# Inverting softmax sums once per query: a row through DRAM in place of four reciprocals on 64 partitions

## The chip, the cores and the metric

The kernel runs on one core of a Trainium2 chip. Its engines are named as in the profile: PE does the matrix products (PEld is its weight load), DVE, ACT and POOL work on tiles in on-chip memory, and each of SP, ACT and POOL can issue DMA transfers. Every engine takes its instructions in the order in which they stand in its own queue. An instruction that waits holds all those behind it on that engine. The metric is device time in microseconds (us) for one execution of the whole layer.

## The reference

One encoder layer runs over 2048 prompt tokens and over 256 sample tokens (18 token tiles of 128). What matters here is the attention half of its mixer. Eight heads of 64 dimensions share two key/value heads, and every query attends to all keys of its own request:

```python
def block(qi):
    s = jnp.einsum('bqhgd,bkhd->bhgqk', qi, k).astype(jnp.float32) * scale
    p = jax.nn.softmax(s, axis=-1)
    return jnp.einsum('bhgqk,bkhd->bqhgd', p.astype(v.dtype), v)
```

Beside it, eight other heads run the mLSTM, a recurrence over chunks of 64 tokens in both directions. The two results go together through `w_out` into the residual, and a gated feed-forward layer with a depthwise convolution follows.

## The kernel before

**Attention in blocks.** `attention` goes over 36 blocks (`hbs`) of 512 queries. A block is named by its first head and first query tile: `1_0` is head 1 from query tile 0. Blocks `0_16`, `2_16`, `4_16` and `6_16` are small ones, for the 256 sample tokens (two heads at once, one pair of key tiles). The other 32 cover the prompt, with eight pairs of key tiles each. The first half of the list (`0_16` to `3_12`) uses key/value head 0, the second half (`4_0` to `6_14`) head 1.

**A pair of key tiles.** `scores` makes the product of keys and queries in a PSUM bank (`ps`, lines 616 and 617). ACT takes the exponential twice, once rounded (`ph`, line 620) and once in full (line 621), and DVE subtracts them into the remainder `pl` (line 622). `values` (line 634) multiplies `ph` and `pl` with the values and adds up over the pairs in one PSUM bank `pv`. The value tiles carry 64 columns of ones, so partitions 64 to 127 of `pv` hold the same softmax sum, 64 times over. `values` lags `scores` by two pairs (`PLAG`). The next block's row maxima are found meanwhile: `maxstep` makes scores (`px`, line 590) that DVE reduces (`mx`, line 591). The banks of `ps`, `px` and two smaller users are shared, four in all (tag `sc`), and `pv` has one buffer.

**The end of a block.** After a block's last pair, `fin1` copies the output (`o1`, line 642) and the 64 copies of the sums (`rs`, line 643) out of `pv` on ACT. `fin2`, four times, inverts 128 columns of `rs` on all 64 partitions (line 651, DVE). `fin3` multiplies the two on POOL (line 655) and stores the result to DRAM (`mix_d`, line 658). `rs` has one buffer, so the next block's `fin1` waits for this block's `fin3`. The six steps stand in the list `fins`; one is taken out after each pair of the next block, two after its last pair, and what is left is flushed ahead of the next `fin1`.

**The mLSTM beside it.** `mlstm` works through four pairs of heads. Its projections are line 780, 790 and (last pair) 808 on PE, from tiles `mn`, `mjn` or `mvn` that SP loads from DRAM (lines 777 and 805) into a ring of eight buffers: a load waits until PE has read the tile that lay there before. Its output steps, one for each of 18 token tiles and each pair of heads, go back and forth between engines: `mS` (PE, line 911), `dm` (DVE, 914), `mI` and `mN` (PE, 917 and 929), `s`, `dn` and `hh` (DVE, 920 to 949, with a square sum on ACT, line 941, and a power on POOL, 104 and 105), `mT` (PE, 954) and `mmx` (957 to 960), which is stored to `mix_d`.

**What sets the order.** `run_both` draws from the two generators by a table of costs. The framework then reorders each engine's queue: it simulates the program with its own idea of durations, and takes the earlier written instruction where several are ready. So a step that it believes shorter can move instructions everywhere in this stretch. Once the mLSTM's generator is exhausted, which falls into block `4_8`, PE's order is taken as written instead: attention and the output projection `phase_c` (`po`, line 1069, from tiles `cmx`) alternate by a fixed pace. After attention follow the feed-forward stages.

Of the kernel before, what the change touches and what calls it, by code (L numbers as in the profile page):

```python
# [9 lines left out]
F32 = mybir.dt.float32  # L10
F32R = mybir.dt.float32r
AF = mybir.ActivationFunctionType
# [5 lines left out]
P = 128  # L18
# [6 lines left out]
HD = 64  # L25
# [468 lines left out]
def attention(g, tc, s1, s2, pp):  # L494


    nc = g.nc
    sp = s1
# [43 lines left out]
    def part(s):  # L542

        t, r = 0, []
        for q in s.qs:
            r.append((t, q))
            t += q[2] - q[1]
        return r
# [77 lines left out]
    def values(s, kp, parts):  # L626

        N = s.N
        if kp == 0:
            s.pv = pp.tile([P, 512], F32, tag="pv", name="pv" + s.nm, bufs=1)  # L630
        vs = [[v[:, (2 * kp + z) % 4, :] for v in s.kv[kp // 2][2]] for z in range(2)]
        todo = [(vs[z][k], parts[z][0]) for z in range(2) for k in range(2)] + [(vs[z][0], parts[z][1]) for z in range(2)]
        for k, (v, p) in enumerate(todo):
            nc.tensor.matmul(s.pv[0:HD if k in (1, 3) else P, 0:N], v, p, start=(kp == 0 and k == 0),  # L634
                             stop=(2 * kp + 2 == s.nk and k == 5))

    def fin1(s):

        N = s.N
        s.o1 = sp.tile([HD, 512], F32, tag="o1", name="o1" + s.nm, bufs=2)  # L640
        s.rs = sp.tile([HD, 512], F32, tag="rs", name="rs" + s.nm, bufs=1)
        nc.scalar.activation(s.o1[:, 0:N], s.pv[0:HD, 0:N], AF.Copy)
        nc.scalar.activation(s.rs[:, 0:N], s.pv[HD:P, 0:N], AF.Copy)
        s.left = list(range(0, N, P))

    def fin2(s):

        if s.left:
            r = s.rs[:, s.left[0]:s.left[0] + P]
            s.left.pop(0)  # L650
            nc.vector.reciprocal(r, r)

    def fin3(s):
        N = s.N
        nc.gpsimd.tensor_tensor(s.o1[:, 0:N], s.o1[:, 0:N], s.rs[:, 0:N], ALU.mult)
        for t0, (h, q0, q1) in part(s):
            r0 = HD * (h % 2)
            nc.gpsimd.dma_start(g.mix_d[q0 // 2:q1 // 2, r0:r0 + HD, 4 + h // 2].rearrange("n p t -> p n t"),
                                s.o1[:, t0 * P:(t0 + q1 - q0) * P].rearrange("p (n t) -> p n t", t=BT))

    def fin4(s):

        for h, q0, q1 in s.qs:
            if h == 7:
                g.mixed.update(range(q0, q1))
# [12 lines left out]
    todo, fins = [], []  # L678

    def value():  # L680

        s, kp, parts = todo.pop(0)
        values(s, kp, parts)
        if kp == s.nk // 2 - 1:
            while fins:
                fins.pop(0)()
            fin1(s)
            fins.extend([lambda: fin2(s)] * 4 + [lambda: fin3(s), lambda: fin4(s)])

    for n in range(len(hbs)):  # L690
        nxt = prep(n + 1) if n + 1 < len(hbs) else None
# [3 lines left out]
        for kp in range(nkp):  # L695
            todo.append((cur, kp, scores(cur, kp)))
            yield 0.4 * A_PAIR
            if ready:
                prep2b(ready)
                ready = None  # L700
            if nxt is not None and nxt.todo:
                if n == len(hbs) // 2 - 1:

                    k = 2 * (kp - 2) - (nxt.nq * nxt.nsp - len(nxt.todo))
                else:
                    k = -(-len(nxt.todo) // max(nkp - kp - (MXZ if g.alone else MXE), 1))
                for i in range(k):
                    maxstep(nxt)
                    if i % 2:
                        yield 2 * A_MAX  # L710
                if not nxt.todo:
                    prep2a(nxt)
                    ready = nxt
            if len(todo) > PLAG:
                value()
                yield 0.6 * A_PAIR
            for _ in range(1 if kp < nkp - 1 else 2):
                if fins:
                    fins.pop(0)()
# [9 lines left out]
    while todo:  # L729
        yield A_PAIR  # L730
        value()
# [866 lines left out]
def body(tc, aps, phases="abcd"):  # L1598
    nc = tc.nc
    g = Ctx()  # L1600
# [3 lines left out]
    with ExitStack() as st:  # L1604
        dp = st.enter_context(tc.tile_pool(name="dram", bufs=1, space=DRAM))
# [5 lines left out]
        def dram(name, shape):  # L1611
            setattr(g, name, dp.tile(shape, F32, name=name))
# [7 lines left out]
        dram("q_d", [NT, P, 8, P])  # L1620
        dram("k_d", [2, P, T])
        dram("v_d", [2, 2, P, NT, HD])
        dram("nm_d", [NT, 17, P])
        dram("og_d", [4, NB, P, 2, P])
        g.ident = kp.tile([P, P], F32, name="ident")
# [177 lines left out]
```

## Time and profile before

| | |
|---|---|
| median of 3 runs | 3366.88 us (3366.43 to 3368.13) |
| profiled execution | 3374.1 us, its span 3372.4 us |
| granted PE clock, mean over the span | 0.986 of full |
| busy share of PE, DVE, ACT, POOL | 97%, 71%, 53%, 39% |
| first and last `rs` copy of attention (line 643) | 252.25 and 1773.25 us |
| copies of `rs` of blocks `1_0`, `6_6`, `4_16`, `6_16`, `4_8` | 377.70, 1368.14, 1374.44, 1421.09, 1465.53 us |

The spans of instructions are the hardware profiler's. PE's instructions overlap one another, so PE can be shown busy while it could take more. "Idle before" is the time that an engine stood still ahead of an instruction, with the instruction that ended it. Times in this document are microseconds unless marked ns.

### The profile page before, as it was taken

The numbers are of one execution on the slowest core, as the hardware profiler recorded it, in microseconds if no ns is written. First come the engines' busy times: TensorE is split into PE (matmuls) and PEld (weight loads), VectorE is DVE, ScalarE is ACT, GpSimd is POOL, SyncE is SP. The second block draws the span as 40 slices with busy tenths as digits, with TensorE's granted clock in tenths as the row PEclk, the third lists the DMA queues.
The fourth block names the chain that finished last, engine by engine and source line by source line (L and its number), as shares of the span: only waits on it lengthen the run. The fifth ranks groups of instructions, "written<-read, shape, count | busy, mean of one in ns | idle before, by whom it ended". The sixth has DMA issues, their size and how long they took to land. (4 is left out here: it accounts for less than half of the span.)

```text
span 3372.4 us, 57131 instructions
## 1 busy us (share of the span) xinstructions
PE 3271.5 (97%) x21366; PEld 3047.6 (90%) x21366; DVE 2403.1 (71%) x3727; ACT 1802.4 (53%) x3781; POOL 1327.6 (39%) x1686
## 2 busy tenths in 40 slices
PE   8899999999999999899999999999999999999998
PEld 6788888888888888788889999999999998999998
DVE  7875687777768788876766778877877776544573
ACT  5545666667666777665552544445555555323331
POOL 8652133213333323211246457645554442851112
PEclk9999999999999999999999999999999999999999
DMA  8765343343336444433347334424322223885563
GB/s 273 229 201 150 94 126 97 105 125 98 113 108 188 130 135 128 123 99 96 103 133 263 129 102 148 127 96 176 107 93 97 100 93 102 302 274 172 164 223 107
DMA packets 300636, 483.03 MB, mean 143 GB/s; under 512 B 36597, under 2 KB 186279, under 8 KB 300359
## 3 DMA queue, kind: packets, MB, share of 16 engines
q1 hardware_dynamic: 247543, 348.34, 32.8%
q0 software_dynamic: 36256, 121.60, 10.8%
q10 hardware_dynamic: 16560, 9.44, 0.9%
q8 instruction: 168, 2.75, 0.3%
q14 instruction: 109, 0.89, 0.1%
HBM read 337.37 MB, written 141.91 MB: 142 GB/s over the span
## 5 line engine op out<-in xcount | busy, mean ns | idle before, releaser
L622 DVE TENSOR_TENSOR pl<-ps,ph 128x512 fp32r<-128x512 f32 x520 | 354.0, 685 | 202.1 <-ACT ps L621 190.3
L1226 PE MATMUL pa<-nt,wut 128*128 128x290 f32 (+1 forms) x3168 | 449.2, 298 | 8.7 <-ACT u L1244 8.6
L620 ACT ACTIVATE ph<-ps 128x512 fp32r<-128x512 f32 x520 | 310.0, 596 | 265.7 <-PE ps L617 253.1
L1226 PEld LDWEIGHTS pa<-nt,wut 128*128 128x128 f32 x3168 | 433.1, 190 | 10.9 <-ACT u L1244 10.6
L591 DVE TENSOR_REDUCE mx<-px 128x1 f32<-128x512 f32 (+1 forms) x528 | 346.5, 674 | 100.0 <-PE px L590 98.0
L1336 DVE SCALAR_TENSOR_TENSOR y<-u,cw,y 128x1152 f32<-128x1152 f32 (+1 forms) x176 | 325.3, 1848 | 39.2 <-ACT yc L1334 17.5
L634 PE MATMUL pv<-ph,v 128*128 128x512 f32 (+1 forms) x1040 | 319.4, 402 | 0.8 <-ACT ph L620 0.3
L621 ACT ACTIVATE ps<-ps 128x512 f32<-128x512 f32 x520 | 310.3, 597 | 0.0
L1555 PE MATMUL et<-tet,wet 128*128 128x384 f32 x1584 | 279.0, 336 | 0.0
L1555 PEld LDWEIGHTS et<-tet,wet 128*128 128x128 f32 x1584 | 277.1, 188 | 0.0
L1069 PEld LDWEIGHTS po<-cmx,wo 128*128 128x128 f32 x1728 | 221.6, 191 | 9.6 <-DVE cmx L1057 1.5
L1069 PE MATMUL po<-cmx,wo 128*128 128x256 f32 x1728 | 225.8, 284 | 1.5 <-DVE cmx L1057 1.3
L1555 PE MATMUL e<-te,we 128*128 128x384 f32 x1188 | 213.9, 341 | 11.0 <-ACT te L1397 7.1
L1555 PEld LDWEIGHTS e<-te,we 128*128 128x128 f32 x1188 | 211.5, 191 | 12.0 <-ACT te L1397 7.3
L616 PE MATMUL ps<-qq,kk 128*128 128x512 f32 x520 | 215.9, 417 | 6.0 <-DVE mx L591 3.8
L780 PE MATMUL mj<-mn,wm 128*128 128x256 f32 x1296 | 200.8, 289 | 9.7 <-DMA mn<-n_d 3.9
L780 PEld LDWEIGHTS mj<-mn,wm 128*128 128x128 f32 x1296 | 185.5, 194 | 26.6 <-issue 6.8
L617 PE MATMUL ps<-qm,kl 65*128 65x512 f32 x520 | 207.6, 401 | 0.0
L590 PE MATMUL px<-kk,qq 128*128 128x512 f32 (+1 forms) x528 | 203.2, 415 | 3.9 <-DVE mx L591 2.6
L790 PEld LDWEIGHTS mv<-wm,mn 128*128 128x128 f32 x1296 | 181.9, 190 | 17.8 <-ACT qb L786 2.3
L790 PE MATMUL mv<-wm,mn 128*128 128x256 f32 x1296 | 194.8, 285 | 0.9 <-ACT qb L786 0.8
L634 PE MATMUL pv<-pl,v 128*128 128x512 f32 x520 | 192.2, 401 | 0.0
(307 smaller groups left out, 7216.9 us busy)
## 6 DMA issues: line engine op xcount, KB each, us to landing
mn<-n_d SPq DMA_DIRECT2D x216, 256.0 KB, 3.4
ru<-w_up SPq DMA_DIRECT2D x88, 512.0 KB, 3.6
a_d<-y POOLq DMA_DIRECT2D x88, 288.0 KB, 2.6
a_d<-tc POOLq DMA_DIRECT2D x66, 288.0 KB, 2.8
n_d<-n1T SPq DMA_DIRECT2D x18, 1024.0 KB, 5.7
dm<-nm_d POOLq DMA_DIRECT2D x72, 256.0 KB, 4.0
mjn<-n_d SPq DMA_DIRECT2D x72, 256.0 KB, 3.5
mvn<-n_d SPq DMA_DIRECT2D x72, 256.0 KB, 3.1
```

Source lines behind the costliest of these rows:

```text
L591: nc.vector.tensor_reduce(s.mx[:, t, z0:z0 + 1], ps[:, 0:w], AX.X, ALU.max)
L616: nc.tensor.matmul(ps, kk[:, kc:kc + P], s.qq[:, 0:N], start=True, stop=False)
L620: nc.scalar.activation(ph, ps, AF.Exp)
L621: nc.scalar.activation(ps, ps, AF.Exp)
L622: nc.vector.tensor_tensor(pl, ps, f32(ph), ALU.subtract)
L634: nc.tensor.matmul(s.pv[0:HD if k in (1, 3) else P, 0:N], v, p, start=(kp == 0 and k == 0), stop=(2 * kp + 2 == s.nk and k == 5))
L780: nc.tensor.matmul(pj[:, o], s.w[c][:, a, o * P:(o + 1) * P], nT[c][:, :, h, :], start=(c + o + k == 0), stop=(c == NCC - 1 and k == 2 and ...
L790: nc.tensor.matmul(pv[:, o], nT[c][:, o, a, :], s.w[c][:, h, 256:512], start=(c + o + k == 0), stop=(c == NCC - 1 and k == 2 and o == 1))
L1069: nc.tensor.matmul(po[:, o], wo[z // 2][c][:, a, n], mx[c][:, h, :], start=(c == 0 and k == 0), stop=(c == NCC - 1 and k == 2))
L1226: nc.tensor.matmul(p[:, z], w[:, aa, c, :], ops[k][:, c, bb, z * m:z * m + m], start=c == 0 and i == 0 and not add, stop=c == NCC // 2 - 1 ...
L1336: nc.vector.scalar_tensor_tensor(y[:, s:e], u[:, s + k:e + k], cw[:, k, jj:jj + 1], y[:, s:e], ALU.mult, ALU.add)
L1555: nc.tensor.matmul(ps[m // 2][:, m % 2], w[:, aa, m * P:(m + 1) * P], t[:, bb], start=p == 0 and n == 0, stop=p == NP - 1 and n == 2)
```

## The change

`fin1` now copies one partition of the sums instead of 64. The four `fin2` steps are replaced by four others. `fin2a` writes the row of 512 sums to DRAM; `fin2b` reads it back as 64 partitions by 8; `fin2c` inverts that tile with one DVE instruction and writes it to a second row in DRAM; `fin2d` reads that row to all 64 partitions of `rs`. The four transfers stand on SP's queue, and each waits for the one before. `fin3` and `fin4` are as they were, and there are again six steps in `fins`. Every block has a DRAM tile of its own (`g.rs_d`, 36 of them).

```diff
         nc.scalar.activation(s.o1[:, 0:N], s.pv[0:HD, 0:N], AF.Copy)
-        nc.scalar.activation(s.rs[:, 0:N], s.pv[HD:P, 0:N], AF.Copy)
-        s.left = list(range(0, N, P))
-
-    def fin2(s):
-
-        if s.left:
-            r = s.rs[:, s.left[0]:s.left[0] + P]
-            s.left.pop(0)
-            nc.vector.reciprocal(r, r)
+        nc.scalar.activation(s.rs[0:1, 0:N], s.pv[HD:HD + 1, 0:N], AF.Copy)
+        s.row = g.rs_d.pop(0)
+
+    def fin2a(s):
+
+        nc.sync.dma_start(s.row[0].unsqueeze(0), s.rs[0:1, :])
+
+    def fin2b(s):
+
+        s.rr = sp.tile([HD, 8], F32, tag="rr", name="rr" + s.nm, bufs=2)
+        nc.sync.dma_start(s.rr, s.row[0].rearrange("(p f) -> p f", f=8))
+
+    def fin2c(s):
+
+        nc.vector.reciprocal(s.rr, s.rr)
+        nc.sync.dma_start(s.row[1].rearrange("(p f) -> p f", f=8), s.rr)
+
+    def fin2d(s):
+
+        nc.sync.dma_start(s.rs, s.row[1].unsqueeze(0).to_broadcast([HD, 512]))
...
-            fins.extend([lambda: fin2(s)] * 4 + [lambda: fin3(s), lambda: fin4(s)])
+            fins.extend([lambda f=f: f(s) for f in (fin2a, fin2b, fin2c, fin2d, fin3, fin4)])
...
+        g.rs_d = [dp.tile([2, 512], F32, name=f"rs_d{k}") for k in range(36)]
```

The change also moves what it does not name, since the framework plans anew. Line numbers behind line 643 are larger by 11 or 12 in the changed kernel (line 808 is its line 819, line 777 its line 788).

On DVE, at the end of block `1_0` (with the first pairs of block `2_0`, and the maxima of block `3_0`), there stood before:

```order
L622 TENSOR_TENSOR pl2_0_0_1_3983<-ps2_0_0_1_3979,ph2_0_0_1_3982 128x512
L877 SCALAR_TENSOR_TENSOR C0_14_2475<-C0_13_2474,dec_137,C0_14_2475 128x65
L591 TENSOR_REDUCE mx3_0_3970<-px3_0_0_0_3987 128x1
L591 TENSOR_REDUCE mx3_0_3970<-px3_0_1_0_3990 128x1
L651 RECIPROCAL rs1_0_4180<-rs1_0_4180 64x128 x4
L591 TENSOR_REDUCE mx3_0_3970<-px3_0_2_0_3993 128x1
L591 TENSOR_REDUCE mx3_0_3970<-px3_0_3_0_3996 128x1
L622 TENSOR_TENSOR pl2_0_1_0_4149<-ps2_0_1_0_4145,ph2_0_1_0_4148 128x512
```

and now:

```order
L591 TENSOR_REDUCE mx3_0_4012<-px3_0_1_0_4032 128x1
L622 TENSOR_TENSOR pl2_0_0_1_4025<-ps2_0_0_1_4021,ph2_0_0_1_4024 128x512
L591 TENSOR_REDUCE mx3_0_4012<-px3_0_2_0_4035 128x1
L591 TENSOR_REDUCE mx3_0_4012<-px3_0_3_0_4038 128x1
L657 RECIPROCAL rr1_0_4270<-rr1_0_4270 64x8
L622 TENSOR_TENSOR pl2_0_1_0_4191<-ps2_0_1_0_4187,ph2_0_1_0_4190 128x512
```

The one small reciprocal stands behind the pair's maxima and ahead of the subtraction of the next pair.

On SP, at the same place, the four transfers of block `1_0` now stand among the loads of the mLSTM's tiles:

```order
L788 DMA mn0_7_0_4620<-n1_d_60 128x512
L648 DMA rs_d3_119<-rs1_0_4222 1x512
L788 DMA mn0_7_1_4621<-n1_d_60 128x512
L788 DMA mn0_7_2_4622<-n1_d_60 128x512
L653 DMA rr1_0_4270<-rs_d3_119 64x8
L788 DMA mn0_7_3_4623<-n1_d_60 128x512
L658 DMA rs_d3_119<-rr1_0_4270 64x8
L788 DMA mn0_7_4_4624<-n1_d_60 128x512
L662 DMA rs1_0_4222<-rs_d3_119 64x512
```

Before, the `mn` loads stood there alone. In 14 of the 36 blocks the four transfers now follow each other with no load between; in the others they have one to nine loads or stores between them.

On PE, at the end of the mLSTM (its last pair of heads, around token tile 10), there stood before, with the scores and maxima of attention between its steps:

```order
L954 MATMUL mT3_10_18303<-ident_118,hh3_10_18033 128x128
L590 MATMUL px4_8_0_1_17226<-kk1_16_4_11391,qq4_8_17193 128x512
L929 MATMUL mN3_13_18308<-va3_6_13674,dm3_13_18009 128x65 x4
L590 MATMUL px4_8_1_1_17229<-kk1_16_4_11391,qq4_8_17193 128x512
L590 MATMUL px4_8_2_1_17273<-kk1_16_4_11391,qq4_8_17193 128x512
L590 MATMUL px4_8_3_1_17276<-kk1_16_4_11391,qq4_8_17193 128x512
L808 MATMUL mv3_8_18247<-mvn3_8_0_18231,wm3_0_13596 128x256 x6
```

and now, with none:

```order
L922 MATMUL mS3_13_18295<-qb3_6_13749,mkT3_6_13748 128x256
L928 MATMUL mI3_13_18299<-C3_13_13725,qb3_6_13749 128x130 x2
L965 MATMUL mT3_10_18391<-ident_154,hh3_10_18121 128x128
L940 MATMUL mN3_13_18396<-va3_6_13750,dm3_13_18097 128x65 x4
L922 MATMUL mS3_14_18415<-qb3_7_13752,mkT3_7_13751 128x256
L928 MATMUL mI3_14_18419<-C3_14_13726,qb3_7_13752 128x130 x2
L819 MATMUL mv3_8_18335<-mvn3_8_0_18319,wm3_0_13672 128x256 x6
```

More of the mLSTM is left for this place. Between the last value product of block `6_6` and that of block `4_8`, PE's queue held 112 projections (line 808), 28 `mN`, 12 `mI`, 6 `mS` and 9 `mT`; it now holds 288, 64, 30, 15 and 18. Between the last subtractions of the same two blocks, DVE's queue held 12 matrices `dm` and 7 sets of `s`, `dn` and `hh` (besides 12 reciprocals of sums); it now holds 34 and 18 (besides 3). From the scores of pair 6 of block `4_8` to the first product of `phase_c`, PE's queue now has 167 instructions of the mLSTM and none of attention. Behind block `4_8`, PE's order in attention is the same in both.

## The prediction

> **What bounds the kernel now.** I read the page's busy shares, then busy times by stage, then PE's waits inside attention.
>
> ```profile
> PE 3271.5 (97%) x21366; PEld 3047.6 (90%) x21366; DVE 2403.1 (71%) x3727; ACT 1802.4 (53%) x3781; POOL 1327.6 (39%) x1686
> ```
>
> The four stages below are cut at the copies of `rs`: the long part of attention from block `0_16` to `6_6`, the end of the mLSTM (to `4_8`) and the densest 47 us in it, then the part in which attention runs with the output projection.
>
> ```profile
> core 0: us, PE busy (x) PEld busy (x) DVE busy (x) ACT busy (x) POOL busy (x), PEclk, DMA share, GB/s
> 252.80:1368.70 1115.90, 1105.64 (x6985) 967.36 (x6984) 829.95 (x1824) 758.60 (x2042) 317.96 (x638) 1.00 0.42 123
> 1368.70:1466.10 97.40, 82.62 (x442) 67.68 (x442) 84.89 (x196) 57.39 (x142) 18.92 (x33) 0.88 0.47 138
> 1383.00:1430.00 47.00, 35.99 (x184) 28.60 (x183) 44.88 (x111) 26.89 (x72) 10.74 (x21) 0.86 0.38 113
> 1466.10:1774.00 307.90, 302.28 (x1900) 264.14 (x1900) 207.60 (x363) 160.74 (x319) 73.86 (x86) 0.99 0.33 102
> ```
>
> PE is busy 99% of the long part, 85% of the 97 us at the mLSTM's end, 98% of the last part. Only in those 97 us does DVE carry the time: in their dense half it is busy 95% (44.88 of 47.00), and PE is idle for 11 us.
>
> From 250 to 1800 us PE waited longest for these three:
>
> ```profile
> PE mj L780 <- DMA mn<-n_d: 3.9, 2, 2.8
> PE ps L616 <- DVE mx L591: 3.8, 2, 3.3
> PE mT L954 <- DVE dn L932: 3.8, 1, 3.8
> ```
>
> Two of the three are DVE's. The next rows of that view are smaller, so the reciprocals' direct cost on PE is a few us.
>
> **What is removed.**
>
> ```profile
> L651 DVE RECIPROCAL rs<-rs x144: 884/887/946, 252.9 to 1776.9; 64x128 f32<-64x128 f32 x144
> sum 1550.00, DVE 121.96; mean DVE 6.78
> ```
>
> The second row is the busy time of line 651 alone between 250 and 1800 us: 121.96 us, 3.4 us a block. What replaces it on DVE is a 64x8 reciprocal; the nearest rows are a 128x4 one and, for ACT's copy of one partition, another 1x512 copy:
>
> ```profile
> L934 DVE RECIPROCAL dn<-dn 128x4 f32<-128x4 f32 x72 | 12.4, 173 | 0.8
> L607 ACT ACTIVATE qm<-pr x36: 573/590/592, 243.2 to 1722.5; 1x512 fp32r<-1x512 f32 x36
> ```
>
> So 36 times about 0.2 us: DVE gets some 115 us back. ACT saves nothing: its copy of 64 partitions took 0.60 too.
>
> **Where a block ends: burst against round trip.** The copy of `rs` in block `1_0`, and what DVE did behind it:
>
> ```profile
> 377.70 0.60 ACT L643 ACTIVATE rs<-pv 64x512 f32<-64x512 f32 x1
> 378.39 3.38 DVE L651 RECIPROCAL rs<-rs 64x128 f32<-64x128 f32 x4 [0.34 <-ACT rs L643]
> 381.70 1.21 DVE L591 TENSOR_REDUCE mx<-px 128x1 f32<-128x512 f32 x2
> 382.83 1.27 DVE L622 TENSOR_TENSOR pl<-ps,ph 128x512 fp32r<-128x512 f32 x2
> ```
>
> Now the reciprocal waits for `fin2a` and `fin2b`. No transfer this small is in the trace; the nearest of SP's are a store of 64 KB and a load of 128 KB (duration on the queue, then issue to landing):
>
> ```profile
> L960 SPq DMA_DIRECT2D mix_d<-mmx x18: 319/326/417, 1292.3 to 1437.9; - x18
> DMA to landing us min/median/max: 1.6/2.4/6.0
> L559 SPq DMA_DIRECT2D bq<-q_d x56: 359/371/1262, 224.7 to 1590.8; - x56
> DMA to landing us min/median/max: 2.2/2.9/6.9
> ```
>
> At the shortest landings the sum is back 0.33 + 1.6 + 0.37 + 2.2 = 4.5 us after the copy, at the medians 6.0. The copy ended at 378.30. By the new order the pair's four maxima are done while DVE waits, so `pl` starts at 378.3 + 4.5 + 0.2 = 383.0 or at 384.5, against 382.83. **DVE's work of 3.4 us has become a wait as long**, in the blocks where the reciprocal stands right behind the first pair: `pl` is 0.2 to 1.7 us later. Behind it on DVE stand only `pl` and `mx`, which free the four score banks that PE needs. Bursts of 3.4 us, with the copy's wait ahead, did not stop PE in the long part (the waits above), so a stall of this size is covered too. Without that cover it would be 25 blocks by 0.2 to 1.7, 5 to 43 us. On the other side DVE is freer in the dense blocks towards 1368 us. I take 0 for the long part, between -10 and +20.
>
> **SP's queue.** All four transfers issue there, 144 in all, each at some 0.35 us, and SP stands still for each landing, some 10 us a block. Behind them queue the `mn` loads. These wait long anyway:
>
> ```profile
> SPq L777 <- PE mv L790: 473.5, 161, 21.0
> ```
>
> 161 waits for PE to free a buffer, up to 21 us, and yet PE waited for `mn` only 3.9 us in all, at the start. Eight buffers in the ring cover it: 0. If they did not, it would cost what the last load is late, up to 10 us in each of the 15 blocks where loads stand between the transfers ahead of block `6_6`.
>
> **POOL.** Its product of `o1` and `rs` waits for the fourth transfer, about 10 us behind the copy instead of 4. What stands behind it is the mLSTM's power `mr` and the masks of `dm`:
>
> ```profile
> POOL o L655 <- DVE rs L651: 104.1, 13, 34.5
> DVE hh L947 <- POOL mr L105: 23.9, 29, 2.6
> ```
>
> POOL stood here up to 34.5 us before, and DVE waited for `mr` 23.9 us in all. 0 again; with the cover gone a few us for each block that has `mr` behind it.
>
> **What the new plan moves.** Here I see the two large terms. PE's pace, from two rows of its timeline:
>
> ```profile
> 1307.21 2.44 PE L808 MATMUL mv<-mvn,wm 128*128 128x256 f32 x19
> 1299.60 1.00 PE L929 MATMUL mN<-va,dm 128*128 128x65 f32 x8
> ```
>
> Less the 0.27 by which the last one's end lags, a projection takes 0.12 and an `mN` 0.10. Behind block `6_6` now stand 176 more projections (21 us), 36 more `mN` and 36 more of `mI`, `mS` and `mT` at about the same (7 us): 28 us of PE work that the long part sheds. PE being its bound, the long part ends **28 us** sooner (20 if it isn't quite full, 31 if its busy time includes gaps).
>
> This work must be done at the mLSTM's end, where DVE sets the pace. An output step costs DVE:
>
> ```profile
> L914 DVE TENSOR_TENSOR dm<-dm,mS 128x256 f32<-128x256 f32 x144 | 53.4, 413 | 5.0 <-PE mS L911 4.4
> L920 DVE TENSOR_TENSOR s<-mI,tm 128x260 f32<-128x260 f32 x72 | 30.4, 422 | 4.6 <-PE mI L917 3.9
> L930 DVE TENSOR_TENSOR s<-mN,s 128x260 f32<-128x260 f32 x72 | 30.1, 419 | 13.1 <-PE mN L929 12.4
> L935 DVE TENSOR_TENSOR s<-s,dn 128x256 f32<-128x256 f32 x72 | 30.8, 428 | 1.3
> L938 DVE TENSOR_TENSOR hh<-s 128x128 f32<-128x128 f32 x72 | 20.8, 289 | 0.7
> L947 DVE TENSOR_TENSOR hh<-hh,mr 128x128 f32<-128x128 f32 x72 | 26.7, 371 | 25.5 <-POOL mr L105 23.9 <-ACT ps L621 0.9
> ```
>
> Two `dm`, the five others and three small ones like the 128x4 reciprocal: 3.3 us. Eleven more steps are 36, less nine of the old reciprocals at 0.85, 28 more. DVE's instructions overlap by a tenth (two maxima in 1.21 above), so its 84.89 busy us become about 110. At 95% busy, as in the dense half, the stage takes 116 us; at its present 87%, 126. Against it stands that 167 instructions of the mLSTM now have no attention among them. There PE meets waits like these:
>
> ```profile
> 1404.15 0.45 PE L954 MATMUL mT<-ident,hh 128*128 128x128 f32 x1 [3.78 <-DVE dn L932]
> 1406.27 1.94 PE L929 MATMUL mN<-va,dm 128*128 128x65 f32 x8 [1.67 <-DVE mmx L959]
> 1405.00:1410.00 5.00, 3.73 (x17) 3.59 (x17) 4.20 (x16) 2.55 (x11) 0.95 (x2) 0.50 0.46 120
> ```
>
> 5.5 us of waits for one step, and half the clock behind it (0.50 in the last row). Seven such steps would be 38 us with PE nearly idle, in place of 23 at DVE's pace, which puts the stage at up to 141 us. I take 125: **+28**, between +19 and +44.
>
> **The last part.** Its PE idle is 307.90 - 302.28 = 5.6 us at most to win; the reciprocals' 27 us on DVE are gone and the transfers have a whole pair's time: **-2**, between -5 and +2. The feed-forward behind it is only shifted: 0.
>
> **Sum.** -28 + 0 + 28 - 2 = -2 against the profiled execution's 3374.1 us (span 3372.4 and 1.7 around it): 3372. That execution lies 7.2 us above the median of the runs, 3366.88, and I carry the difference over: **3365 us**.
>
> **Rivals.** *The mLSTM's end absorbs the work.* The stage already has PE idle for 14.8 us and 12% of its clock lost, 26 us together; projections fill just such holes. At the saturated 116 us, with 8 us of DVE relief won in the dense blocks ahead: -28 - 8 + 19 - 2 = -19, 3348. For it: the projections are what those holes lacked. Against: the lone steps behind them. *The round trip stops PE.* In the long part, `pl` is late by 1 us in each of 25 blocks, and PE, with four score banks, feels two thirds of it: +17, so +15 and 3382. It decides once the landings reach the medians above while DVE has nothing left to do ahead of the reciprocal. Against: PE did not feel the bursts. *The lone steps run at their chain's latency.* Stage of 138 us, +13 more: 3378. *PE was never full.* PEld was busy 87% of the long part, PE 99%; if PE's busy time hides that it followed DVE, half of the 25 bursts of 3.4 us comes off: -42 more, 3323. The Trainium skill ("Perfetto Trace Analysis", Identifying the Most-Contended Engine) says that matmul busy time overstates PE and that weight-load busy time is the better measure. This trace bears it out only in the gap of 87 to 99; the waits on DVE do not.
>
> **How the numbers follow.** Forecast 0.38, absorbed 0.30, round trip 0.18, latency 0.10, never full 0.04. The forecast's own range is 3358 to 3373. What a measurement tells from no change is 0.2%, 6.7 us: below 3360, above 3374. Of the forecast 0.28 is no change, 0.07 faster, 0.03 slower; of the absorbed case 0.26 is faster, the rest no change; round trip and latency are slower but for 0.03 together. So faster 0.37, no change 0.35, slower 0.28. The range of 3345 to 3383 leaves out the never-full case and the edges of two others.
>
> **What would show it.** Right: the copies of `rs` of block `6_6` some 28 us earlier, the stage from there to `4_8` near 125 us with DVE over 85% busy and a stretch without `pl` at its end; the line of the small reciprocal with idle time of 1 to 3 us ahead of each. Wrong: PE rows that wait for `mx` or `pl` in the long part; `mj` waiting for its tiles; or the stage to `4_8` under 115 us.

## The result, and the profile after

The changed kernel takes 3382.28 us (median; 3379.89 to 3385.42), the kernel before 3366.65 beside it. The ratio is **1.0044, 95% interval 1.0033 to 1.0056**: 15.6 us slower, where 3365 was forecast and a slower kernel had a chance of 0.28. The time lies at the upper end of the range, where the rival "the round trip stops PE" stood. A second set on another chip gave 1.0054 (1.0037 to 1.0071).

The busy shares of the changed kernel's page. DVE lost 97 us of work (2403.1 before; some 115 were forecast), PE nothing:

```profile
PE 3271.2 (97%) x21366; PEld 3049.8 (90%) x21366; DVE 2306.0 (68%) x3619; ACT 1803.2 (53%) x3781; POOL 1326.8 (39%) x1686
```

Its busy times by stage, cut at the copies of `rs` as in the forecast (long part, the mLSTM's end, last part):

```profile
core 0: us, PE busy (x) PEld busy (x) DVE busy (x) ACT busy (x) POOL busy (x), PEclk, DMA share, GB/s
253.10:1330.05 1076.95, 1065.13 (x6677) 929.20 (x6675) 736.00 (x1647) 738.62 (x1956) 290.16 (x588) 1.00 0.41 120
1330.05:1481.09 151.04, 127.48 (x751) 109.91 (x751) 106.44 (x288) 78.16 (x228) 43.44 (x85) 0.86 0.57 168
1481.09:1785.00 303.91, 300.32 (x1906) 264.18 (x1905) 185.98 (x342) 160.63 (x319) 73.31 (x85) 1.00 0.34 106
```

The long part is 39.0 us shorter (1115.9 before), the mLSTM's end 53.6 longer (97.4), the last part 4.0 shorter (307.9). With 0.3 at the start that is 11.0 of the 11.3 us between the two profiled spans. The rest up to 15.6 is how far the two profiled executions lie above their medians (7.4 before, 3.1 now).

308 PE records left the long part with 40.5 us of busy time, and 309 came back at the mLSTM's end with 44.9. By line they are the work that the new plan moves: 180 projections left and 179 came, with 72 and 74 records of `mN`, 36 of `mI`, 18 of `mS` and 9 of `mT`; a few of other lines go the other way. (The trace shows each `mN`, `mI` and `mS` of the program as two records.) What is lost at the mLSTM's end is 8.8 us more of idle PE (151.04 - 127.48 against 97.40 - 82.62) and 4.4 in which the same work took longer, at a granted clock of 0.86 (0.88 before). DVE is busy there 70% (106.44 of 151.04), not above 85% as I forecast: it no longer carries the stage.

**The stretch without attention.** From the last matmul of attention to the mLSTM's last one, and 10 us inside it (views by window):

```profile
1401.50:1450.80 49.30, 36.36 (x221) 30.89 (x219) 33.48 (x110) 23.09 (x81) 14.81 (x31) 0.81 0.50 154
1440.00:1450.00 10.00, 5.27 (x18) 3.56 (x17) 6.18 (x23) 2.31 (x14) 2.80 (x6) 0.50 0.12 36
```

The 221 PE records (of the 167 instructions in the queue, each `mN`, `mI` and `mS` being two) take 49 us, no engine is busy above three quarters, and in the last 10 us PE has 18 records at half its clock.

**The round trip.** SP's queue and the two waits in block `1_0` of the changed kernel (timeline; lines 648, 653, 658 and 662 are the four transfers):

```profile
367.33 0.59 ACT L643 ACTIVATE rs<-pv 1x512 f32<-1x512 f32 x1
367.95 0.24 SPq L648 DMA_DIRECT2D rs_d<-rs  x1
369.87 0.46 SPq L653 DMA_DIRECT2D rr<-rs_d  x1
372.81 0.20 DVE L657 RECIPROCAL rr<-rr 64x8 f32<-64x8 f32 x1 [2.66 <-DMA rr<-rs_d]
373.04 0.47 SPq L658 DMA_DIRECT2D rs_d<-rr  x1
374.75 0.46 SPq L662 DMA_DIRECT2D rs<-rs_d  x1
378.17 1.27 POOL L666 TENSOR_TENSOR o<-o,rs 64x512 f32<-64x512 f32 x1 [8.57 <-DMA rs<-rs_d]
```

The small reciprocal starts 4.9 us after the copy's end, POOL's product 10.3 after. Over the 36 blocks it is 3.0 to 15.4 (median 4.35) and 7.8 to 20.2 (median 10.2). The forecast had 4.5 to 6.0 and about 10. In the long part the waits are (view of waits: engine, line, releaser; us in all, times, longest):

```profile
POOL o L666 <- DMA rs<-rs_d: 199.6, 22, 24.3
DVE rr L657 <- DMA rr<-rs_d: 42.3, 21, 8.8
```

So DVE stands still 2.0 us ahead of each of 21 reciprocals, of the size that was forecast (1 to 3 us). I had called that, and POOL's wait, free.

### The profile page after: what moved, and what is told of

The parts are those of the page before. It is cut to its first block, busy times and chain, and to the rows that moved or that the text cites. A ratio compares the mean times of both kernels' runs of the same rounds, so it can differ in the third digit from the quotient of the medians.

```text
span 3383.7 us, 57263 instructions
## 1 busy us (share of the span) xinstructions
PE 3271.2 (97%) x21366; PEld 3049.8 (90%) x21366; DVE 2306.0 (68%) x3619; ACT 1803.2 (53%) x3781; POOL 1326.8 (39%) x1686
## 5 line engine op out<-in xcount | busy, mean ns | idle before, releaser
L634 PEld LDWEIGHTS pv<-ph,v 128*128 128x128 f32 (+1 forms) x1040 | 157.7, 163 | 37.4 <-ACT ph L620 1.2
```

## The experiments

I held two theories. PLAN: the transfers cost nothing, the reordered work does. ROUND TRIP: the waits cost, the order is neutral. Each needs one run without the other's cause. All ratios are to the kernel before on the same chip.

**norec: no reciprocals, no transfers.**

```diff
-            nc.vector.reciprocal(r, r)
+            pass
```

> The kernel before with the four reciprocals of a block left out (the softmax sums are not inverted, so attention is multiplied by its sums) and nothing put in their place: no transfer, no wait. Two theories for the 15.6 us that the change cost. PLAN: the transfers cost nothing that PE feels; without the reciprocals' work on DVE the planner draws attention ahead, 154 PE instructions of the mLSTM's end stand without attention, and that stretch runs at the latency of its chain. Then this kernel is as slow as the changed one, 3375 to 3385 us, with 140 to 155 us from the copy of rs of 6_6 to that of 4_8. ROUND TRIP: DVE and SP stand still for the transfers and PE pays for it. Then this kernel, without them, is 3350 to 3367 us.

Measured: 1.0003 (0.9993 to 1.0014), 3368.6 us, 1.6 above what ROUND TRIP allowed and 6 below what PLAN asked for. PLAN falls as stated: the plan is almost that of the changed kernel, with the stretch, and costs nothing in sum. Nor did leaving out the reciprocals gain anything. Windows of `norec` (blocks `3_12` to `6_6`, `6_6` to `4_8`, the stretch):

```profile
973.80:1321.60 347.80, 344.14 (x2144) 298.27 (x2143) 255.10 (x584) 245.67 (x663) 96.67 (x196) 1.00 0.44 131
1321.60:1457.30 135.70, 119.50 (x752) 104.19 (x752) 105.08 (x287) 77.92 (x227) 42.78 (x82) 0.91 0.62 183
1387.80:1429.60 41.80, 30.49 (x204) 26.33 (x204) 31.97 (x105) 20.96 (x75) 14.13 (x29) 0.86 0.50 153
```

The same two stretches of the changed kernel:

```profile
975.20:1330.00 354.80, 347.49 (x2146) 299.57 (x2144) 250.66 (x591) 246.61 (x662) 95.88 (x195) 1.00 0.44 131
1330.00:1481.10 151.10, 127.54 (x752) 109.97 (x751) 106.44 (x288) 78.20 (x229) 43.49 (x85) 0.86 0.57 168
```

In these two executions, with the same number of PE records, the first is 7.0 us longer with the round trip and the second 15.4. (The profiled execution of `norec` lies 9.5 us below its median, so these sizes are upper ones; the ratios differ by 0.0041, 14 us.) From `0_16` to `3_12`, `norec` takes 723.2 and the changed kernel 722.1: no loss shows there.

**dum and dum2: the transfers under the plan of before.**

```diff
+    def idle(s, k):
+        r = s.rs[32:HD, k * P:(k + 1) * P]
+        nc.vector.reciprocal(r, r)
...
         nc.sync.dma_start(s.row[0].unsqueeze(0), s.rs[0:1, :])
+        idle(s, 0)
```

and so in each of the four steps.

> The changed kernel with four reciprocals of 128 columns added again per block, on 32 partitions of rs ahead of the fourth transfer (work that no output needs; the sums are copied on 64 partitions for it, as before). All transfers and their waits stay. The new order is nearly that of the kernel before: 159 PE instructions of the mLSTM behind block 6_6, one alone at the end. PLAN: 3362 to 3372 us, 95 to 105 us from 6_6 to 4_8. ROUND TRIP: it has the transfers' waits and the old bursts, so 3382 us or more.

> dum once more, beside side_pw on one chip and for a second profile: with the plan of before, the transfers, POOL's wait for them and four reciprocals that nobody needs. It took 1.0037 of before; 3374 to 3384 us again. If it comes out at 3366 to 3371, its first result was the chip's, and the transfers cost nothing under the plan of before.

Measured: 1.0037 (1.0024 to 1.0050) and 1.0025 (1.0013 to 1.0038). With nearly the old order, and with the old bursts as well, the round trip costs 8 to 12 us. That is less than ROUND TRIP asked for and more than PLAN allowed. DVE's wait is short in both, 14.9 and 14.0 us in nine and eight blocks, where the changed kernel has 50.9 us in 27, because the old burst stands ahead of the small reciprocal. POOL's wait is not short: 235.4 and 207.8 us, against 245.6.

**lead12 and b_lead12: mLSTM spread over more blocks.** LEAD is how far `run_both` lets the mLSTM be ahead of attention, by its table of costs.

```diff
-LEAD = 1.3
+LEAD = 1.2
```

> The changed kernel with LEAD 1.2 in place of 1.3, so that attention is drawn earlier and the mLSTM's end is spread among three more blocks: 506 PE instructions of the mLSTM behind 6_6, with 324 of attention among them, 7 alone at the end. PLAN: the stretch without attention is gone, 3360 to 3371 us. ROUND TRIP: transfers as in the changed kernel, 3378 to 3386 us.

> The kernel before with LEAD 1.2, the control of lead12. Its order has 167 PE instructions of the mLSTM behind 6_6 and 1 alone, as with 1.3. Both theories: 3361 to 3372 us. If it gains as much as lead12 does, LEAD has an effect of its own that has nothing to do with the change.

Measured: 1.0023 (1.0014 to 1.0033), and the control 1.0089 (1.0076 to 1.0102). `lead12` lies between the two theories, and both missed with the control: LEAD 1.2 costs the kernel before 30 us. So it does not tell the two apart.

**after2, nodve, nopool: which wait?** `after2` is the changed kernel again. In the other two:

```diff
-        nc.vector.reciprocal(s.rr, s.rr)
```

```diff
-        nc.scalar.activation(s.rs[0:1, 0:N], s.pv[HD:HD + 1, 0:N], AF.Copy)
+        nc.scalar.activation(s.rs[:, 0:N], s.pv[HD:P, 0:N], AF.Copy)
...
-        nc.sync.dma_start(s.rs, s.row[1].unsqueeze(0).to_broadcast([HD, 512]))
+        s.rz = sp.tile([HD, 64], F32, tag="rz", name="rz" + s.nm, bufs=1)
+        nc.sync.dma_start(s.rz, s.row[1][0:64].unsqueeze(0).to_broadcast([HD, 64]))
```

> The changed kernel once more, on the chip of the three that follow, for their comparison and for a second profile of it. 3379 to 3386 us, 9 to 20 above the kernel before. If the stage from 6_6 to 4_8 takes 145 us or more again, its length is no accident of one execution.

> The changed kernel without the small reciprocal (the sums are not inverted): the third transfer stores what the second one read. SP's four transfers and POOL's wait for the fourth stay; DVE waits for nothing. The plan is nearly that of the changed kernel (424 PE instructions of the mLSTM behind 6_6, 221 alone at the end; 415 and 167 there). The run without reciprocals and transfers gave 1.0003 of the kernel before, the run with both 1.0037, so the transfers cost 12 to 15 us; three theories of where. DVE'S WAIT (50.9 us in 27 blocks ahead of the reciprocal): gone here, so 3364 to 3372 us. POOL'S WAIT (245.6 us in 31 blocks ahead of its product, with the loads of dm and ogT and the power mr behind it): still 3378 to 3388. SP'S QUEUE (the mn loads behind the transfers): still 3378 to 3388.

> The changed kernel with the sums copied on 64 partitions as before, and POOL's product with this copy (not inverted). The four transfers and the small reciprocal stay, but the fourth reads only 64 of the 512 values, into a tile that nobody reads, so POOL waits only for ACT. The plan has 418 PE instructions of the mLSTM behind 6_6, 215 alone at the end. POOL'S WAIT: 3364 to 3372 us. DVE'S WAIT and SP'S QUEUE: 3378 to 3388.

Measured: 1.0054 (1.0037 to 1.0071), 1.0047 (1.0032 to 1.0062), 1.0048 (1.0034 to 1.0063). The stage is long again in `after2` (146.4 us). Neither wait alone gives anything back, which read by itself would point to SP's queue. But each edit moved the order again: the stretch without attention is 62.6 us in `nodve` and 59.3 in `nopool`, 49 in the changed kernel. The comparison is spoilt by that and decides nothing.

**mend0 and its control: a shorter stretch.** M_END is how much of the mLSTM's end, by the table of costs, `run_both` draws in one piece, without attention.

```diff
-M_END = 16
+M_END = 0
```

> The changed kernel with M_END 0 in place of 16, so that the mLSTM's last steps are written among attention instead of in one piece: the same 415 PE instructions of the mLSTM behind 6_6, but 179 of attention among them (115 before) and 63 alone at the end instead of 167. If the stretch without attention costs what my forecast put on it (about 0.2 us for each of 104 instructions, PE nearly idle), 3362 to 3372 us. If the time is set by the transfers alone, 3378 to 3386.

> The kernel before with M_END 0, the control of mend0. Its plan keeps 167 PE instructions of the mLSTM behind 6_6 and 1 alone, so there is no stretch to fill: 3364 to 3372 us. If it gains 5 us or more, M_END 0 helps for another reason than the stretch without attention.

Measured: 1.0025 (1.0014 to 1.0037), 6 to 10 us faster than the changed kernel and between the two expectations. The stretch of `mend0`:

```profile
1425.60:1455.40 29.80, 18.75 (x91) 15.28 (x91) 20.57 (x70) 12.01 (x48) 11.31 (x21) 0.65 0.38 107
```

The control came out at 1.0036 (1.0023 to 1.0050), slower, not equal. In it the output projection starts at 1459.87 instead of 1440.01. So M_END 0 has a cost of its own in that order and no hidden benefit. The gain in `mend0` fits the shorter stretch (29.8 us, 49.3 in the changed kernel), less what M_END 0 itself may cost there, which no run separates.

**The waits again, with M_END 0.** The same edits on `mend0`, whose plans are now much alike (37 to 87 instructions alone). `free_M0` has both edits, `norec_M0` is `norec` with M_END 0.

> The kernel before without its reciprocals (the sums are not inverted), no transfers, and M_END 0: the plan of mend0 (415 PE instructions of the mLSTM behind 6_6, 180 of attention among them, 41 alone at the end). The run without reciprocals and with M_END 16 gave 3368 us; M_END 0 took 7 us off the changed kernel. If the stretch without attention costs the same here, 3357 to 3364 us, which is then what the reciprocals' work on DVE is worth at most. If M_END matters only beside the transfers, 3365 to 3371.

> nopool (POOL does not wait for the transfers, which run) with M_END 0: 418 PE instructions of the mLSTM behind 6_6 with 169 of attention among them, 63 alone, the same as mend0, whose POOL waits and which took 1.0025 of before. nopool itself had 215 alone against 167 of the changed kernel, which may have hidden what it saved. POOL'S WAIT: 3364 to 3370 us, like norec_M0 (0.9993). Otherwise as mend0, 3375 to 3379.

> nodve (the small reciprocal left out, POOL waits) with M_END 0: 424 PE instructions of the mLSTM behind 6_6, 169 of attention among them, 87 alone. POOL'S WAIT: as mend0, 3374 to 3380 us. DVE'S WAIT: 3364 to 3370.

> mend0 without both waits: no small reciprocal (as nodve_M0), and POOL's product with a copy on 64 partitions (as nopool_M0); the sums are not inverted. The four transfers run, nobody on DVE or POOL waits for them. 415 PE instructions of the mLSTM behind 6_6 with 180 of attention among them, 37 alone, as in norec_M0. If the waits are all that the transfers cost: 3364 to 3370 us, as norec_M0 (0.9993) and nodve_M0 (1.0004). If SP's queue or the traffic costs something under this plan, as nopool_M0, 3374 to 3380.

| M_END 0 | transfers | DVE waits | POOL waits | ratio |
|---|---|---|---|---|
| norec_M0 | no | no | no | 0.9993 (0.9983 to 1.0003) |
| free_M0 | yes | no | no | 1.0014 (1.0004 to 1.0025) |
| nodve_M0 | yes | no | yes | 1.0004 (0.9994 to 1.0014) |
| nopool_M0 | yes | yes | no | 1.0022 (1.0013 to 1.0031) |
| mend0 | yes | yes | yes | 1.0025 (1.0014 to 1.0037) |

`norec_M0` and `nopool_M0` came out at one of their two expectations (3367 and 3378 us), `nodve_M0` and `free_M0` between theirs (3372 both). The two with DVE's wait have a mean of 1.00235, `free_M0` and `nodve_M0` one of 1.0009: 5 us for DVE's wait, uncertain by some 3.5, since each ratio is uncertain by 0.001. The small reciprocals' own work on DVE, 36 by 0.19 us, is in that price. POOL's wait makes no difference that these runs can tell. The transfers without any wait cost 0.0021 (7 us, uncertain by 5), which nothing here explains. `norec_M0` is 3 us below `norec`, with a stretch of 23.4 us instead of 41.8. Read by itself this says that the stretch costs next to nothing without the round trip; a cost of M_END 0 of its own, as in its control, could hide what the shorter stretch saves, and that is not tested. And it sets the ceiling for this order: **inversion at no cost at all would win about 2 us, 6 at best.**

**side: the transfers beside the kernel before.** The old reciprocals stay and give the results; the transfers run as extra work:

```diff
+    def fin2a(s):
+        s.row = g.rs_d.pop(0)
+        nc.sync.dma_start(s.row[0].unsqueeze(0), s.o1[0:1, :])
...
-            fins.extend([lambda: fin2(s)] * 4 + [lambda: fin3(s), lambda: fin4(s)])
+            fins.extend([lambda: (fin2(s), fin2a(s)), lambda: (fin2(s), fin2b(s)), lambda: (fin2(s), fin2c(s)), lambda: (fin2(s), fin2d(s))] + [lambda: fin3(s), lambda: fin4(s)])
```

`side_nodve` leaves out the small reciprocal, `side_pool` issues the transfers from POOL. `side_pw` makes POOL wait:

```diff
+        nc.gpsimd.tensor_copy(s.rs[:, 0:1], s.rz[:, 0:1])
         nc.gpsimd.tensor_tensor(s.o1[:, 0:N], s.o1[:, 0:N], s.rs[:, 0:N], ALU.mult)
```

> The kernel before, with its four reciprocals on 64 partitions and all its results, and beside them the four transfers and the small reciprocal of the change as extra work that nobody reads: the row is taken from o1, and the fourth transfer reads 64 values into a tile of its own. POOL does not wait for it. The plan stays that of before (156 PE instructions of the mLSTM behind 6_6, 1 alone at the end; before 167 and 1). If the transfers cost the 12 us that dum showed, with the plan of before: 3376 to 3384 us. If dum's cost came from POOL's wait alone, 3364 to 3371.

> side without the small reciprocal: the third transfer stores what the second read, and DVE waits for none of them. 168 PE instructions of the mLSTM behind 6_6, 1 alone. DVE'S WAIT as the cost of the transfers: 3364 to 3371 us. SP'S QUEUE or the transfers themselves: as side, 3376 to 3384.

> side with the four transfers issued by POOL instead of SP, so that SP's loads stand behind none of them. DVE still waits for the second. 178 PE instructions of the mLSTM behind 6_6, 1 alone. SP'S QUEUE as the cost: 3364 to 3371 us. DVE'S WAIT: as side, 3376 to 3384; more if POOL's own waits now hold up dm and mr.

> side, in which the transfers and DVE's wait cost nothing (1.0004 of before), with one small POOL instruction ahead of POOL's product: it copies a value of the fourth transfer's tile over column 0 of rs, so that POOL waits for the whole round trip as in the changed kernel (one of 512 columns of the inverted sums is overwritten). 228 PE instructions of the mLSTM behind 6_6, 3 alone. POOL'S WAIT as the cost: 3376 to 3384 us, and POOL's wait for that transfer above 150 us in all. If POOL's wait is free too, 3366 to 3372.

Measured: 1.0004 (0.9994 to 1.0014), 1.0009 (1.0000 to 1.0018), 1.0004 (0.9994 to 1.0015), and with POOL's wait **1.0039 (1.0024 to 1.0054)**. SP's queue and the transfers are free in this order, to within 5 us. The run says little on DVE's wait, though I had meant it to: in `side` the old burst of 3.4 us stands ahead of the small reciprocal and covers most of it, so that DVE waits only 10.4 us, in six blocks. POOL's wait costs 12 us (uncertain by 6), and `dum` and `dum2`, in which POOL waits and DVE hardly does, lie 11 and 7 us above `side`. The order of `side_pw` is not quite that of before, though: 228 PE instructions of the mLSTM stand behind `6_6`, 156 in `side`, and the added copy takes POOL 0.18 us in each block. POOL's waits ahead of its product in `side`, then in `side_pw`:

```profile
POOL o L675 <- DVE rs L651: 104.2, 13, 30.3
```

```profile
POOL rs L675 <- DMA rz<-rs_d: 232.5, 26, 24.2
```

And the mLSTM's end (`6_6` to `4_8`) in `side`, then in `side_pw`:

```profile
1370.30:1465.70 95.40, 81.90 (x433) 65.15 (x433) 85.57 (x200) 58.53 (x146) 21.23 (x36) 0.89 0.48 141
```

```profile
1357.20:1473.70 116.50, 93.33 (x516) 75.73 (x516) 93.36 (x224) 61.45 (x160) 26.47 (x47) 0.90 0.48 141
```

Of the 21 us more, 11.4 are PE work that the order moved in (83 records), 9.7 are idle PE.

**How a wait on POOL reaches PE.** The changed kernel in block `6_2`, whose copy of `rs` ended at 1164.9 (timeline, the rows of the chain):

```profile
1171.79 0.20 DVE L657 RECIPROCAL rr<-rr 64x8 f32<-64x8 f32 x1 [3.50 <-DMA rr<-rs_d]
...
1177.60 1.28 POOL L666 TENSOR_TENSOR o<-o,rs 64x512 f32<-64x512 f32 x1 [5.93 <-DMA rs<-rs_d]
...
1180.66 0.72 POOL L105 TENSOR_TENSOR mr<-mr,mhalf 128x2 f32<-128x2 f32 x1
...
1181.42 0.29 DVE L958 TENSOR_TENSOR hh<-hh,mr 128x128 f32<-128x128 f32 x1 [3.53 <-POOL mr L105]
1181.62 0.68 DVE L591 TENSOR_REDUCE mx<-px 128x1 f32<-128x512 f32 x1
...
1182.37 1.39 PE L590 MATMUL px<-kk,qq 128*128 128x512 f32 x2 [2.80 <-DVE mx L591]
```

The late reciprocal makes the fourth transfer late, POOL's product waits 5.93 for it, the mLSTM's `mr` stands behind the product and its stores, DVE waits 3.53 for `mr`, the maxima stand behind that on DVE, and PE has no free bank for 2.80. The same wait of PE is in the second profile (3.92 us) and in `mend0` (3.45); in `norec`, `nodve` and `nopool` PE has no wait above 1 us in this block. DVE's wait and POOL's are two links of one chain here, so their prices need not add.

## Why the prediction was wrong

**Right.** PE is the bound of the long part; DVE's relief by itself is worth nothing that these runs can tell (`norec`, `norec_M0`). The work moves behind `6_6`, and the long part and the stage balance: the forecast's sum of -2 would be 0.9994, inside the interval of `norec`. That the two terms cancel is the mechanism. That their sum came out so near is partly luck, since neither size was right: in the profile of `norec` the long part is 45 us shorter and the stage 38 longer, where I had 28 for each. The rival by which PE was never full (3323 us) is out: without the reciprocals nothing is gained, although weight loads were busy only 87% of the long part. The Trainium skill ("Perfetto Trace Analysis", Identifying the Most-Contended Engine) would have the weight loads judge that; here PE's waits judged better. (The section says that matmul busy time is not a good measure of how close a kernel is to its peak; that it overstates PE was my wording.)

**Wrong, first: the round trip put at nothing ("burst against round trip", 0 between -10 and +20).** The sum has 0 for it here, 0 for SP's queue, 0 for POOL, and no term at all for the three blocks that end between `6_6` and `4_8`. The runs price it at 14 to 17 us (the changed kernel less `norec`) and 11 (`mend0` less `norec_M0`). The stalls were as long as forecast, though the sum for them was not right: "issue to landing" counts from the start of the issuing instruction, so 0.33 and 0.37 went in twice. Without that the sum is 3.8 to 5.3, and 4.35 was the median. What failed is the cover. I took it from the bursts: a stall of 3.4 us on DVE did not stop PE before, so one as long would not now. But behind a burst POOL's product can follow at once, while behind this wait stand two more transfers: the product now starts 10.2 us after the copy (median), and what stands behind it on POOL, later still. Block `6_2` shows one path from there to PE; that such paths make up the whole loss is argued, not shown.

Where the loss falls is less clear. From `3_12` to `6_6`, profiles with both waits take 354.8, 356.0 and 354.5 us (changed kernel twice, `mend0`), those without one or both 346.5 to 351.8, with 2143 to 2148 PE records in each. From `0_16` to `3_12` it is the other way, 721.7 to 722.3 against 721.9 to 727.8, so that over the long part 1076.1 to 1078.4 stand against 1069.1 to 1079.6. A loss in the long part is thus not shown, and my 0 for that part alone may stand within its bounds. From `6_6` to the last copy of `rs` the changed kernel takes 454.3 us and `norec` 439.5, `mend0` 441.2 and `norec_M0` 432.9: the larger part of the loss stands there. So the rival "the round trip stops PE" had the right time, 3382, by luck: it put two thirds of 1 us into each of 25 blocks of the long part.

**Wrong, second: "POOL. 0 again".** The step named what stands behind the product, `mr` and the masks of `dm`, and a price of a few us for each block with `mr` behind it "with the cover gone". In an order near that of before POOL's wait costs some 7 to 12 us (`side_pw`, `dum`, `dum2`); I gave it no chance among the rivals. With M_END 0 no cost of it shows.

**Mis-sized: the stage from `6_6` to `4_8`, +28, measured +53.6 and, in the second profile, +49.0.** 11 of it is not a loss: the long part shed 39 instead of 28. The matmuls are those that I counted, the price was wrong. I took 0.10 us for an `mN` from eight records, and an `mN` is two (576 records for 72 steps with four each; so with `mI` and `mS`). My 248 instructions are 311 records, and 308 left, with 40.5 us: less 21 for the projections, that is 19 us for the rest, for which I had 7. What remains of the excess, 15 and in the second profile 11, is idle PE and slower PE work; `norec`, with the same work and no round trip, has +38 here. I had the stage at DVE's pace and kept the lone steps' latency as a rival of 138 us. The stretch alone took 49 us, for which the bound of 141 had 38, and the waits of the round trip in the three blocks that end here were not in the sum. How the 15 us divide between these two is not shown.

**SP's queue, 0:** right to within 5 us under the order of before (`side`, `side_pool`).

**What the steps come to.** From 1.0044 to 1.0054 for the changed kernel, M_END 0 takes 0.0019 to 0.0029 off (6 to 10 us), leaving out the small reciprocal 0.0021 more (7 us), and what is left, 1.0004 with POOL still waiting, is no difference. This is one path through the runs; another gives other parts. **Open** is the split of the round trip's 11 to 17 us (`mend0` less `norec_M0`, the changed kernel less `norec`) between DVE's wait, POOL's and the traffic: with M_END 0 it came out as 5, 0 and 7, in orders near that of before as 7 to 12 for POOL's wait and 0 for the traffic, with DVE's wait hardly tested. No version here beats the kernel before.

## What to carry to other kernels

Before giving an engine relief, take its work out without replacement and time that: here the ceiling was 2 us, 6 at best, so a replacement with waits had next to nothing to win. A wait on an in-order engine is paid by whatever stands behind it, so follow the chain through the second engine (POOL's product, `mr`, DVE, PE) before calling it covered; what covered a burst need not cover a wait that a second engine shares. Where a planner sets the order, compare experiments only after comparing their orders, and don't treat two costs as alternatives if both can stand in one stage.

## What the runs showed of the hardware

PE's clock fell without a long gap. The granted clock (PEclk, the third figure from the end) in short windows of the changed kernel, then its PE rows at the end of the stretch:

```profile
1432.00:1434.00 2.00, 1.08 (x8) 0.97 (x8) 2.00 (x7) 1.59 (x5) 1.25 (x2) 1.00 0.70 196
1434.00:1436.00 2.00, 1.47 (x6) 1.07 (x6) 1.90 (x6) 1.62 (x4) 0.00 (x0) 0.85 0.58 167
1436.00:1438.00 2.00, 0.76 (x3) 0.22 (x2) 2.00 (x6) 0.63 (x1) 0.00 (x0) 0.50 0.08 13
```

```profile
1421.30 0.71 PE L928 MATMUL mI<-C,qb 128*128 128x130 f32 x4
...
1431.18 0.30 PE L965 MATMUL mT<-ident,hh 128*128 128x128 f32 x1 [0.52 <-DVE dm L925]
1432.41 1.08 PE L940 MATMUL mN<-va,dm 128*128 128x65 f32 x8 [0.93 <-DVE s L931]
1434.44 0.70 PE L922 MATMUL mS<-qb,mkT 128*128 128x256 f32 x2 [0.95 <-ACT qb L847]
1435.23 1.11 PE L928 MATMUL mI<-C,qb 128*128 128x130 f32 x4
1438.17 1.97 PE L940 MATMUL mN<-va,dm 128*128 128x65 f32 x8 [1.40 <-DVE s L931]
```

Four `mI` take 0.71 us at 1421 and 1.11 at 1435, eight `mN` 1.08 at 1432 and 1.97 at 1438. The three waits ahead of that were 0.52, 0.93 and 0.95. The Trainium skill ("TensorE: Matmul & The Clock Gate", Why this matters for your kernels) warns of gaps above about 3 us; here the clock went from 1.00 to 0.50 behind three below 1 us within 4 us, with none above 1 us since 1408. So idle time in a latency chain can cost more than its own length. The mean clocks fit that (0.988 for the kernel before beside `after2`, 0.984 for `after2`), but no run separates this share of the loss.
